# A hybrid decoder step: the input stage in another order, xT stored in parts, the scratch read back in four transfers

## The chip, the core and the metric

The kernel runs on one core of a Trainium2 chip. The metric is the device time of one execution in microseconds (us). Three runs of the kernel before give the time; one further execution was recorded by the hardware profiler, and all rows below come from that one. TensorE multiplies, VectorE (DVE), ScalarE (ACT) and GpSimd (POOL) do the elementwise work, SyncE (SP) issues most transfers; an engine works through its instructions in the order in which they were written. PSUM is the memory that TensorE writes.

## What is computed

One layer of a decoder for 256 prompt rows and 8 sample rows that share all weights, in float32:

```python
h = rmsnorm(x, norm_mix)
proj = h @ w_in                       # q, k, v, z, pooling input, two gates, decays
pool_out = pool_mixer(proj[...])      # trailing window means, 4 groups
qkv = silu(short_conv(proj[...]))     # causal depthwise conv, 4 taps
o = gated_delta_chunked(q, k, v, g, beta, state)
merged = gate_pool * (pool_out @ w_pool_up) + gate_gdn * (o_gated @ w_gdn_up)
x = x + merged @ w_o
gu = rmsnorm(x, norm_ffn) @ w_gate_up
x = x + (silu(gu[..., :D_FF]) * gu[..., D_FF:]) @ w_down
x = x + (p_l @ w_ple) * sigmoid(x @ w_ple_gate)
y = rmsnorm(x, norm_final)
```

The model width is 2048, with 16 heads of 128; the outputs are y for both groups and the new pooling, conv and delta-rule states.

## The kernel before

**Layout.** Activations are held transposed: 128 channels on the partitions, 16 such tiles (`KT`), and 264 columns, the 256 prompt rows and the 8 sample rows. Each float32 product is made of three fast ones: both operands are split into a high part (`wh`, `hh`) and a rest (`wl`, `hl`), and high by high, high by rest and rest by high are summed in PSUM.

**Weights.** `stream` lists all weight blocks in order, 512 KB each. `wload` (L431) issues the transfer of the next into one of three `wr` buffers on SP; `wsplit` (L443) has ScalarE copy it to `wh` and VectorE, or GpSimd when the planner finds it free, subtract to `wl`; four buffers of each. `wblock` (L457) hands the next split block to a gemm. `gemm` (L471) runs over blocks, and between its products calls `tick`.

**Order.** All order is written by the program. `Model` (L34) keeps an estimated time for each engine while the instructions are generated, and `tick` (L260) advances other work, in the form of generators, when the estimate says that its data is there: `paced` ones at every tick, `main` one after another, `post` and `lanes` side by side. A generator that yields -1 is resumed when the estimate of its last work is reached, one that yields a tuple at that time. `Model.run` adds 7 us to a large transfer that ScalarE issues (L147).

**Input.** `load_x` (L616) issues x in seven pieces, the sample rows, and the first three weight blocks. `input_norm` (L632) transposes 16 groups of channels (`xt` in PSUM, copied to `xT`), with the squares of each quarter of x on ScalarE and VectorE after the group's second transpose. Then VectorE sums them, GpSimd takes the power (L383), TensorE spreads the factor over the columns (`rb`) and ScalarE copies it to `rx`. `htile` (L670) makes one tile: VectorE multiplies to `xn`, ScalarE copies to `hh`, VectorE subtracts to `hl`; the last one also issues the store of all of `xT` to DRAM (`xd`, read again as the residual much later). One weight block and four tiles are made ahead of the first gemm, the rest inside it.

**First gemm and conv.** `qkv` (L796) with `wide` set makes the keys of the first four heads with four PSUM banks at a time, 8 blocks of 24 products; the next gemm makes the queries. After each the generator steps `a` (ScalarE: last tap, and the rows for the state), `b` (VectorE: the other taps) and `d` (SiLU) read the bank, so it comes free when the taps are done. `conv_state` (L580) prepares the sample rows' conv and at its end copies two rows of the state from DRAM to DRAM.

**Delta rule.** For each of four head groups `gdn_a` (L871) builds triangular matrices and inverts their diagonal blocks on GpSimd. It writes 32x32 blocks to DRAM (`scr`, four transfers of 32 KB on ScalarE's queue), reads them back to `gone` four times over (L970, one transfer of 512 KB), runs 62 steps on GpSimd, and moves the result by way of `scr2` to `Tt`. `gdn_b` follows. `gdn_sample` (L1148) does the sample rows, with `swap` (L1188) storing each state and loading another. `pool_state` (L1329) loads old pooling rows and copies 14 of 15 from DRAM to DRAM, `p_rows` (L1558) loads the rows of p; each transposes at the next resumption. `ffn` (L1521) holds the longest stretch of plain gemms.

Of the kernel before, what the change touches and what calls it, by code (L numbers as in the profile page):

```python
# [14 lines left out]
P = 128  # L15
# [18 lines left out]
class Model:  # L34
# [92 lines left out]
    def run(self, floor=0.0):  # L127
# [5 lines left out]
        for k in range(self.seen, len(lst)):  # L133
            i = lst[k]
            eng = str(i.engine).split(".")[-1]
            if eng not in self.T or type(i).__name__.startswith("Bass"):
                continue
            ins = [b for b in map(self.box, i.ins) if b]
            out = [b for b in map(self.box, i.outs) if b]
            at = max([self.T[eng], floor] + [self.ready(b) for b in ins])  # L140
            if type(i).__name__ == "InstDMACopy":
                self.T[eng] = at + 0.06
                n = max(self.free(b) * (b[2] - b[1]) for b in ins + out) * 4
                end = max(self.ring, at) + n / 320e3
                self.ring = end
                end += 2.3
                if eng == "Activation" and n > 200000:  # L147
                    end += 7.0
                store = out and out[0][5] is None and out[0][0].startswith("out_")
                self.stored = end if store else getattr(self, "stored", 0.0)  # L150
                for b in out:
                    self.wrote(b, end)
                if not store:
                    done = max(done, end)
                continue
            held, more = self.cost(i, ins, out)
            self.T[eng] = at + held
            end = at + held + more
            for b in out:
                self.wrote(b, end)  # L160
            done = max(done, end)
# [4 lines left out]
class Step:  # L166
# [276 lines left out]
    def wsplit(self):  # L443
# [8 lines left out]
        self.sub(lo, raw, hi.bitcast(F32), self.nc.gpsimd if spare else None)  # L452
# [18 lines left out]
    def gemm(self, K, xh, xl, evac, wide=None):  # L471
        M, KS = (2, KB) if wide is None else (4, 2)
        for m0 in range(0, 4, M):
# [7 lines left out]
            for k0 in range(0, K, KS):  # L481
                nk = min(KS, K - k0)
                wh, wl = self.wblock()
                for m in range(M):
                    if wide is not None:
                        if m % 2 == 0 and k0 + 4 + m // 2 < K:
                            self.htile(k0 + 4 + m // 2)
                        elif (m == 1 or k0 > 7) and m % 2 and len(self.pre) < 3:
                            if not self.raws:
                                self.wload()  # L490
                            self.wsplit()
# [88 lines left out]
    def conv_state(self):  # L580
# [32 lines left out]
        self.dma(o["conv_s"][0, :, 0:2, :], i["state_conv"][0, :, 1:3, :])  # L613
# [18 lines left out]
    def input_norm(self, x, xs):  # L632
# [6 lines left out]
        for c in range(4):  # L639
            for k in range(4 * c, 4 * c + 4):  # L640
                t = self.ps("xt")[:, :NT]
                for b in range(2):
                    self.tr(t[:, b * P:(b + 1) * P], x[:, b, k * P:(k + 1) * P])
                cc = (k % 8) * P
                self.tr(t[:, TP:NT], xs[k // 8][:, cc:cc + P])
                if k % 4 == 3:
                    nc.vector.tensor_copy(self.xt[:, k], t)
                else:
                    self.copy(self.xt[:, k], t)
                if k % 4 == 1:  # L650
                    cs = slice(c * 512, c * 512 + 512)
                    xc = (c % 2) * 512
                    self.act(sqj[:, :512], x[:, 0, cs], AF.Square, accum_out=ssq[:, 0, c:c + 1])
                    self.stt_sum(sqj[:, 512:1024], x[:, 1, cs], ssq[:, 1, c:c + 1])
                    self.stt_sum(sqj[:NS, 512:1024], xs[c // 2][:, xc:xc + 512], ssq[:NS, 2, c:c + 1])
# [3 lines left out]
        self.powr(r, r, -0.5)  # L659
        p = self.spread_rows(r)  # L660
        self.rx = self.e1("rx")
        self.copy(self.rx, p)
        self.hh = self.B3("hh", F32R)
        self.hl = self.B3("hl", F32R)

    def stt_sum(self, out, a, acc):
        self.nc.vector.scalar_tensor_tensor(out=out, in0=a, scalar=1.0, in1=a, op0=ALU.mult, op1=ALU.mult,
                                            accum_out=acc)

    def htile(self, k):  # L670
        t = self.e1("xn")
        self.stt(t, self.xt[:, k], self.g_mix(k), self.rx, ALU.mult, ALU.mult)
        self.split(self.hh[:, k], self.hl[:, k], t)
        if k == KT - 1:
            self.dma(self.xd, self.xt)
# [120 lines left out]
    def qkv(self, part, hg, dst, wide=None):  # L796
# [5 lines left out]
        def evac(m, ps):  # L802
# [3 lines left out]
            u = ps  # L806
            tap = lambda r: self.stt(y[:, 3 - r:TP], u[:, 0:TP - 3 + r], w(r), y[:, 3 - r:TP])
# [17 lines left out]
            self.then(a, b, d, bank=True)  # L825
# [45 lines left out]
    def gdn_a(self, hg, q, k):  # L871
# [94 lines left out]
        for d in range(4):  # L966
# [3 lines left out]
        self.fast(at.rearrange("p s c -> p (s c)"),  # L970
                  scr.rearrange("d a s c -> (d a) (s c)").unsqueeze(0).broadcast_to([4, 32, 1024]))
# [176 lines left out]
    def gdn_sample(self, pool):  # L1148
# [39 lines left out]
        def swap(hg, h):  # L1188
            self.dma(o["ssm_s"][0, :, hg * GH + h].rearrange("b d e -> d b e"), S.pop((hg, h)))
# [139 lines left out]
    def pool_state(self):  # L1329
# [3 lines left out]
        self.dma(o["pool_s"][0, :, 0:14, :], i["state_pool"][0, :, 1:15, :])  # L1333
        yield -1
# [185 lines left out]

    def ffn(self):  # L1521
        nc = self.nc
        self.lane(self.rbcast())
        for g0, ng in ((0, 4), (4, 4), (8, 3)):
# [33 lines left out]
    def p_rows(self):  # L1558
# [5 lines left out]
        yield -1  # L1564
# [84 lines left out]
    def run(self):  # L1649
# [6 lines left out]
        self.wsplit()  # L1656
        for k in range(4):
            self.htile(k)
# [89 lines left out]
```

## Time and profile before

| | before |
|---|---|
| median of 3 runs | 1960.99 us (1959.58 to 1961.83) |
| the profiled execution | 1956.55 us |
| its span | 1954.8 us |
| TensorE busy in the span | 1887.4 us (97%), 15700 matmuls |
| VectorE, ScalarE, GpSimd busy | 1121.1, 877.3, 523.8 us |
| moved by DMA | 344.92 MB, mean 176 GB/s |
| mean granted TensorE clock | 0.985 |

The span is the time between the first and the last recorded instruction; the profiled execution's own time is 1.75 us longer, and the median of the runs shown 4.4 us longer still. Matmuls overlap, so a busy TensorE is not one at its best pace: the number of matmuls that a stretch holds says more. Times in rows are us from the span's start, durations of single groups in the group view are ns. What stands in brackets behind a row is the idle time of that engine just before it and what ended it.

### The profile page before, as it was taken

To read this page: it belongs to the slowest core of one execution; us is meant where nothing else is said; L and a number is where in the kernel's file an instruction comes from. 1 tells how busy PE (TensorE), PEld (TensorE's weight loads), DVE (VectorE), ACT (ScalarE), POOL (GpSimd) and SP (SyncE) were. 2 spreads that over 40 slices of the span, in tenths; PEclk is the share of its full clock that TensorE was granted. 3 is DMA by queue.
4 is the path that set the end of the run, shared out by engine and by line. 5 is a ranking of instruction groups with operands and counts; after the bars stand their busy time and mean duration, and the time that the engine had idled before them with its cause. 6 is when DMAs were issued, how large, how long until landed. Compare 5 with 4: busy or idle time off the path is not lost.

```text
span 1954.8 us, 38004 instructions
## 1 busy us (share of the span) xinstructions
PE 1887.4 (97%) x15700; PEld 1856.6 (95%) x15700; DVE 1121.1 (57%) x1592; ACT 877.3 (45%) x1478; POOL 523.8 (27%) x562
## 2 busy tenths in 40 slices
PE   7789999999999899999999999999999999999997
PEld 5788999999999889999999999999999999999997
DVE  5556557565545966556565555544555545557554
ACT  3454455556544343354354344433444333444444
POOL 1244526363602643412132111100111101113111
PEclk9899999999999999999999999999999999999998
DMA  4546646474657668865655655555655555655553
GB/s 142 170 130 155 179 122 175 129 186 114 189 141 220 179 202 266 247 181 173 212 183 173 185 187 183 180 182 176 188 181 180 183 185 174 184 181 178 168 169 123
DMA packets 367568, 344.92 MB, mean 176 GB/s; under 512 B 26034, under 2 KB 362747, under 8 KB 367251
## 3 DMA queue, kind: packets, MB, share of 16 engines
q1 hardware_dynamic: 354003, 338.82, 57.8%
q10 hardware_dynamic: 13392, 3.67, 1.0%
q8 instruction: 123, 2.02, 0.4%
q14 instruction: 50, 0.41, 0.1%
HBM read 327.28 MB, written 16.03 MB: 176 GB/s over the span
## 4 chain that ended last, share of the span: by engine, by line
PE 81%; DVE 6%; DMA 4%; ACT 4%; issue 2%; POOL 2%; ACTq 0%; SPq 0%; POOLq 0%; DVEq 0%
PE acc L370 75%; DVE wl L341 2%; ACT wh L357 2%; DMA wr<-in_w_in_dram 2%; POOL wl L341 1%; DVE db L341 1%; DMA gone<-scr 1%; DMA wr<-in_w_o_dram 1%; PE pp L370 1%; ACT gset L354 0%; PE kqp L1236 0%; POOL rm L344 0%; PE py L370 0%; PE px L370 0%; DVE dpl L351 0%
## 5 line engine op out<-in xcount | busy, mean ns | idle before, releaser
L341 DVE TENSOR_TENSOR wl<-wr,wh 128x1024 fp32r<-128x1024 f32 x488 | 615.8, 1275 | 571.2 <-ACT wh L357 570.4
L357 ACT ACTIVATE wh<-wr 128x1024 fp32r<-128x1024 f32 x594 | 611.5, 1049 | 483.4 <-PE acc L370 171.7
L370 PE MATMUL acc<-hh,wh 128*128 128x264 f32 x1664 | 490.0, 294 | 18.1 <-DVE k L347 9.3
L370 PE MATMUL acc<-hh,wl 128*128 128x264 f32 x1664 | 479.0, 288 | 12.8 <-POOL wl L341 8.3
L370 PE MATMUL acc<-hl,wh 128*128 128x264 f32 x1664 | 478.8, 288 | 0.0
L341 POOL TENSOR_TENSOR wl<-wr,wh 128x1024 fp32r<-128x1024 f32 x106 | 260.7, 2462 | 738.0 <-ACT wh L357 489.3
L370 PE MATMUL acc<-xnh,wh 128*128 128x264 f32 x1408 | 399.9, 284 | 0.0
L370 PE MATMUL acc<-xnh,wl 128*128 128x264 f32 x1408 | 399.1, 283 | 0.0
L370 PE MATMUL acc<-xnl,wh 128*128 128x264 f32 x1408 | 399.1, 283 | 0.0
L370 PEld LDWEIGHTS acc<-hh,wh 128*128 128x128 f32 x1664 | 320.1, 192 | 22.8 <-issue 11.6
L370 PEld LDWEIGHTS acc<-hh,wl 128*128 128x128 f32 x1664 | 318.9, 192 | 15.1 <-POOL wl L341 9.6
L370 PEld LDWEIGHTS acc<-hl,wh 128*128 128x128 f32 x1664 | 320.1, 192 | 1.5 <-DVE hl L341 0.4
L370 PEld LDWEIGHTS acc<-xnl,wh 128*128 128x128 f32 x1408 | 265.1, 188 | 0.0
L370 PEld LDWEIGHTS acc<-xnh,wh 128*128 128x128 f32 x1408 | 264.9, 188 | 0.0
L370 PEld LDWEIGHTS acc<-xnh,wl 128*128 128x128 f32 x1408 | 264.4, 188 | 0.0
L370 PE MATMUL acc<-hidh,wh 128*128 128x264 f32 x704 | 199.9, 284 | 0.0
L370 PE MATMUL acc<-hidl,wh 128*128 128x264 f32 x704 | 199.6, 283 | 0.0
L370 PE MATMUL acc<-hidh,wl 128*128 128x264 f32 x704 | 199.5, 283 | 0.0
L370 PEld LDWEIGHTS acc<-hidl,wh 128*128 128x128 f32 x704 | 132.5, 188 | 0.0
L370 PEld LDWEIGHTS acc<-hidh,wh 128*128 128x128 f32 x704 | 132.4, 188 | 0.0
L370 PEld LDWEIGHTS acc<-hidh,wl 128*128 128x128 f32 x704 | 132.2, 188 | 0.0
L344 POOL TENSOR_TENSOR gs<-gs,rb 128x264 f32<-128x264 f32 x44 | 33.3, 757 | 365.8 <-ACT gs L354 365.7
(362 smaller groups left out, 2727.7 us busy)
## 6 DMA issues: line engine op xcount, KB each, us to landing
wr<-in_w_in_dram SPq DMA_DIRECT2D x208, 512.0 KB
wr<-in_w_gate_up_dram SPq DMA_DIRECT2D x176, 512.0 KB
wr<-in_w_down_dram SPq DMA_DIRECT2D x88, 512.0 KB
wr<-in_w_gdn_up_dram SPq DMA_DIRECT2D x32, 512.0 KB
wr<-in_w_o_dram SPq DMA_DIRECT2D x32, 512.0 KB
wr<-in_w_ple_gate_dram SPq DMA_DIRECT2D x32, 512.0 KB
S<-in_state_ssm_dram SPq DMA_DIRECT2D x16, 512.0 KB
out_dram<-S SPq DMA_DIRECT2D x16, 512.0 KB
```

The lines of the kernel that those rows point to most:

```text
L341: (eng or self.nc.vector).tensor_tensor(out=out, in0=a, in1=b, op=ALU.subtract)
L344: (eng or self.nc.vector).tensor_tensor(out=out, in0=a, in1=b, op=ALU.mult)
L357: self.nc.scalar.activation(out, a, AF.Copy)
L370: self.nc.tensor.matmul(out, lhsT, rhs, start=start, stop=stop)
```

## The change

Six parts. (1) `input_norm` puts the squares of a quarter ahead of its transposes (the last quarter's ahead of transpose 10), transposes 12 groups, then computes the factor with two weight splits and transposes 12 and 13 around it; the first two splits go to GpSimd by name. Four tiles and a third split follow; transposes 14 and 15 go inside the first gemm, which now splits one block ahead per block. (2) `htile` puts the subtract of a tile behind the multiply and copy of the next. (3) The store of `xT` is a lane of eight transfers, one per 10 us of the planner's time. (4) In the wide gemm ScalarE copies each bank to `u` in SBUF, and the conv reads that. (5) The readback of `scr` is four transfers to 32 partitions each, and the planner's 7 us are gone. (6) The two state copies go to a lane in `ffn`; `swap` waits in the planner's time for the state that it stores; `pool_state` and `p_rows` resume 12 us after their loads.

```diff
@@ Model.run
-                if eng == "Activation" and n > 200000:
-                    end += 7.0
@@ wsplit
-    def wsplit(self):
+    def wsplit(self, eng=None):
...
-        self.sub(lo, raw, hi.bitcast(F32), self.nc.gpsimd if spare else None)
+        self.sub(lo, raw, hi.bitcast(F32), self.nc.gpsimd if spare else eng)
@@ gemm
                     if wide is not None:
-                        if m % 2 == 0 and k0 + 4 + m // 2 < K:
+                        if m % 2 == 0 and k0 + 4 + m // 2 <= K:
                             self.htile(k0 + 4 + m // 2)
-                        elif (m == 1 or k0 > 7) and m % 2 and len(self.pre) < 3:
+                        if m == 1 and k0 < 4:
+                            self.turn(14 + k0 // 2)
+                        if m == 1:
                             if not self.raws:
                                 self.wload()
                             self.wsplit()
@@ conv_state
-        self.dma(o["conv_s"][0, :, 0:2, :], i["state_conv"][0, :, 1:3, :])
@@ input_norm
-        for c in range(4):
-            for k in range(4 * c, 4 * c + 4):
...
-                if k % 4 == 1:
...
+        self.turn = turn
+        for k in range(12):
+            if k in (0, 4, 8):
+                squares(k // 4)
+            if k == 10:
+                squares(3)
+            if k == 8:
+                self.wsplit(nc.gpsimd)
+            turn(k)
         r = self.cp.tile([P, 3], F32, name="rin")
         nc.vector.tensor_reduce(r, ssq, axis=AX.X, op=ALU.add)
         self.ts(r, r, 1.0 / D, EPS, ALU.mult, ALU.add)
         self.powr(r, r, -0.5)
+        self.wsplit(nc.gpsimd)
+        turn(12)
         p = self.spread_rows(r)
+        turn(13)
         self.rx = self.e1("rx")
         self.copy(self.rx, p)
...
+        for k in range(2):
+            self.htile(k)
+        self.wsplit()
+        for k in range(2, 4):
+            self.htile(k)
@@ htile
-        t = self.e1("xn")
-        self.stt(t, self.xt[:, k], self.g_mix(k), self.rx, ALU.mult, ALU.mult)
-        self.split(self.hh[:, k], self.hl[:, k], t)
-        if k == KT - 1:
-            self.dma(self.xd, self.xt)
+        last = self.xn
+        if k < KT:
+            t = self.e1("xn")
+            self.stt(t, self.xt[:, k], self.g_mix(k), self.rx, ALU.mult, ALU.mult)
+            self.copy(self.hh[:, k], t)
+            self.xn = k, t
+        if last:
+            self.sub(self.hl[:, last[0]], last[1], self.hh[:, last[0]].bitcast(F32))
+    def stow(self):
+        for a in range(0, KT, 2):
+            yield (self.now + 10.0,)
+            self.dma(self.xd[:, a:a + 2], self.xt[:, a:a + 2])
@@ qkv
             u = ps
+            if wide:
+                u = self.e1("u")
+                self.copy(u, ps)
...
-            self.then(a, b, d, bank=True)
+            self.then(a, b, d, bank=not wide)
@@ gdn_a
-        self.fast(at.rearrange("p s c -> p (s c)"),
-                  scr.rearrange("d a s c -> (d a) (s c)").unsqueeze(0).broadcast_to([4, 32, 1024]))
+        for c in range(4):
+            self.fast(at[32 * c:32 * c + 32].rearrange("p s c -> p (s c)"), scr.rearrange("d a s c -> (d a) (s c)"))
@@ gdn_sample, swap
+            yield self.at(S[hg, h])
@@ pool_state
-        self.dma(o["pool_s"][0, :, 0:14, :], i["state_pool"][0, :, 1:15, :])
-        yield -1
+        yield (self.now + 12.0,)
@@ ffn
+    def states(self):
+        i, o = self.i, self.o
+        yield (self.now + 60.0,)
+        self.dma(o["conv_s"][0, :, 0:2, :], i["state_conv"][0, :, 1:3, :])
+        yield (self.now + 60.0,)
+        self.dma(o["pool_s"][0, :, 0:14, :], i["state_pool"][0, :, 1:15, :])
...
+        self.lane(self.states())
@@ p_rows
-        yield -1
+        yield (self.now + 12.0,)
@@ run
-        self.wsplit()
-        for k in range(4):
-            self.htile(k)
+        self.lane(self.stow())
```

## Rows read from the trace of the kernel before

**Rows 1.** Windows: stretch, length, busy us (instructions) of PE, PEld, DVE, ACT, POOL; clock, DMA share, GB/s.

```profile
25.00:50.00 25.00, 21.47 (x139) 19.78 (x140) 17.78 (x30) 9.97 (x18) 4.85 (x3) 0.93 0.47 129
50.00:75.00 25.00, 13.76 (x100) 13.07 (x100) 17.40 (x27) 10.66 (x20) 7.61 (x4) 0.80 0.65 229
175.00:200.00 25.00, 19.31 (x134) 18.58 (x132) 12.44 (x18) 9.88 (x18) 11.87 (x23) 0.86 0.65 149
1300.00:1325.00 25.00, 25.00 (x209) 25.00 (x208) 11.17 (x12) 9.55 (x9) 0.00 (x0) 1.00 0.57 176
```

**Rows 2.** Waits of TensorE, whole span: who for whom, us in total, times, longest.

```profile
PE acc L370 <- DVE k L347: 9.3, 1, 9.3
PE gc L370 <- DVE dg L347: 5.4, 1, 5.4
...
PE pt L374 <- DMA prompt_p<-in_p_prompt_dram: 2.0, 1, 2.0
...
PE spt L374 <- DMA sprow<-in_state_pool_dram: 1.6, 1, 1.6
```

**Rows 3.** Timeline, 0 to 30 us: start, duration, engine, line, operation, tiles.

```profile
12.04 0.69 DVE L667 SCALAR_TENSOR_TENSOR sqj<-x 128x512 f32<-128x512 f32 x1 [0.50 <-DMA x<-in_x_prompt_dram]
...
16.25 0.69 PE L374 MATMUL xt<-ident,x 128*128 128x128 f32 x2
...
17.07 0.69 PE L374 MATMUL xt<-ident,x 128*128 128x128 f32 x2
...
18.79 0.85 POOL L383 TENSOR_TENSOR rin<-rin,mhalf 128x3 f32<-128x3 f32 x1 [17.41 <-DVE rin L351]
...
19.69 1.75 PE L370 MATMUL rb<-ident,rin 128*128 128x128 f32 x6 [1.74 <-POOL rin L383]
...
24.98 0.59 PE L370 MATMUL acc<-hh,wh 128*128 128x264 f32 x1 [3.54 <-ACT hh L357]
```

**Rows 4.** Timeline of VectorE and GpSimd in the first gemm.

```profile
30.27 0.43 DVE L341 TENSOR_TENSOR hl<-xn,hh 128x264 fp32r<-128x264 f32 x1 [0.49 <-ACT hh L357]
...
31.27 2.35 POOL L341 TENSOR_TENSOR wl<-wr,wh 128x1024 fp32r<-128x1024 f32 x1 [9.56 <-ACT wh L357]
...
31.60 2.31 DVE L341 TENSOR_TENSOR hl<-xn,hh 128x264 fp32r<-128x264 f32 x1 [0.49 <-ACT hh L357]
...
35.75 1.22 DVE L341 TENSOR_TENSOR wl<-wr,wh 128x1024 fp32r<-128x1024 f32 x1 [0.51 <-ACT wh L357]
```

**Rows 5.** Waits of TensorE, 0 to 160 us.

```profile
PE acc L370 <- POOL wl L341: 5.1, 3, 1.9
```

**Rows 6.** Timeline, 52 to 72 us: SP's queue, ScalarE and TensorE.

```profile
52.66 0.50 SPq L363 DMA_DIRECT2D xd<-xT  x1
...
65.23 1.06 ACT L357 ACTIVATE wh<-wr 128x1024 fp32r<-128x1024 f32 x1 [6.37 <-DMA wr<-in_w_in_dram]
66.20 0.46 ACT L360 ACTIVATE k<-acc,cw 128x264 f32<-128x264 f32 x1
...
71.36 0.56 PE L370 MATMUL acc<-hh,wh 128*128 128x264 f32 x1 [9.32 <-DVE k L347]
```

**Rows 7.** Windows, 55 to 60 us, columns as in rows 1.

```profile
55.00:60.00 5.00, 5.00 (x41) 4.88 (x40) 4.02 (x5) 2.81 (x4) 2.41 (x1) 1.00 1.05 428
```

**Rows 8.** Timeline, 172 to 278 us: the scratch's transfers and who waits for them.

```profile
172.10 1.87 ACTq L367 DMA_DIRECT2D scr<-gset  x4
...
175.71 1.36 ACTq L367 DMA_DIRECT2D gone<-scr  x1
...
188.97 0.24 POOL L344 TENSOR_TENSOR gset<-gone 128x31 f32<-128x31 f32 x1 [9.86 <-DMA gone<-scr]
...
189.73 1.06 ACT L357 ACTIVATE wh<-wr 128x1024 fp32r<-128x1024 f32 x1 [9.16 <-DMA wr<-in_w_in_dram]
...
234.92 0.39 ACTq L367 DMA_DIRECT2D scr<-gone  x1
...
277.26 0.55 ACTq L367 DMA_DIRECT2D gone<-scr  x1
```

## What was predicted

> **What bounds the kernel now.** I read the windows of the engines first. In a stretch of the later matrix stages TensorE is busy all 25.00 us and issues 209 instructions, so one matmul of 264 columns takes 25/209 = 0.12 us and nothing but fewer or faster matmuls would help there [rows 1]. The change adds and removes no matmul, so all it can win is time in which TensorE does not run at that pace. The same view shows where that is: the stretch from 25 to 75 us (13.76 of 25.00 busy in its second half, with a mean granted clock of 0.80), and 175 to 200 us (19.31 busy, clock 0.86) [rows 1]; and nothing of the large products runs in the first 24.98 us [rows 3]. Then I read who TensorE waited for. Four rows touch what is edited: 9.3 us in one wait for the conv taps on VectorE (tile k), 5.4 us in one wait for the decay chain (dg), 2.0 us for prompt_p and 1.6 us for the pool state rows [rows 2]. Last come the timelines of the first 72 us and of the readback of the scratch, which say what was late in each place.
>
> **Input stage.** Before, the 16 transpose groups come first (the last begins at 17.07, one every 0.82), the power on GpSimd starts at 18.79 and takes 0.85, the broadcast takes TensorE 1.75 from 19.69, and the first product of the large gemm starts at 24.98 [rows 3]. After, the last squares stand ahead of the transposes 10 and up, and only 12 groups stand ahead of the factor. What then sets the factor is the arrival of x and GpSimd's order. The third quarter of x lets VectorE start its squares at 12.04, at 0.69 each [rows 3], so two pairs of squares end at 12.04 + 4 x 0.73 = 14.9 if the last quarter is there by 13.4, which no row shows; 17.07 - 3 x 0.82 = 14.6, when transpose 13 began unhindered, is its latest, and that gives 16.1. The power, however, is now queued behind a weight split on GpSimd, 2.35 us each [rows 4], that starts after a ScalarE copy of 1.06 [rows 6] behind the squares of quarter three: 12.04 + 0.69 + 1.06 = 13.8, so GpSimd is free at 16.1. The same split holds up VectorE: while GpSimd ran one from 31.27, a VectorE subtract that took 0.43 just before took 2.31 [rows 4]. If the squares are held up in that way the power starts at about 18.5, if not at 16.4. I take 17.8. Behind it stand 0.85 for the power, 1.75 for the broadcast, 0.82 for transpose 13, two ScalarE copies and three small steps of about 0.4 each: 5.1 us, so the first product starts at 22.9 (21.5 to 23.7), **2.1 us** earlier (1.2 to 3.5).
>
> **First gemm.** It runs from 24.98 to 71.36 - 9.32 = 62.04, 37.1 us, for 192 products that need 192 x 0.12 = 23.0. TensorE waits 5.1 us in it, three times, for weight splits on GpSimd [rows 5], because one block only is split ahead; in the window 25 to 50 it issues 139 instructions of a possible 209, 8.4 us lost, 1.75 of them by the clock (0.93 is half speed for 3.5 us) [rows 1]. With three blocks split ahead (8.6 us of products) a split of 2.35 on GpSimd or 1.22 on VectorE no longer ends last, and with the subtract of a tile put behind the next multiply VectorE does not idle for ScalarE. VectorE then carries per block of 24 products (2.9 us) two tiles of two steps, about 0.4 each as in the subtract's 0.43, and one split at 1.22 [rows 4], 2.8 us in all: just under TensorE, so not all the loss goes. I give back 5.0 of 8.4 (0 to 8.4) and charge 2 x 0.82 = 1.6 for transposes 14 and 15, which now lie inside the gemm: **+3.4 us** (-1.6 to 6.8).
>
> **The stall behind it.** xT's store (2.1 MB) is issued at 52.66 with 384 KB of state copy behind it, and the DMA engines run at 428 GB/s with a share of 1.05 from 55 to 60 [rows 6, 7]. The weight block queued behind them lets ScalarE go on only at 65.23 after 6.37 idle, the conv's first step follows at 66.20, and TensorE gets its banks at 71.36 [rows 6]. After, the store is 8 transfers of 264 KB, 10 us apart on the planner's clock, each 264/428 = 0.6 us of the engines beside a weight stream that leaves room; the state copies go to the feed-forward stage, where TensorE is at its 209 and DMA at a share of 0.57 [rows 1]. SP issues each part when xT has long been written, so nothing waits behind it. The banks are released by one copy of 0.46 per bank on ScalarE instead of by the taps on VectorE. What is late next is that copy behind one weight copy: 0.46 + 1.06 = 1.5. So 9.3 - 1.5 = 7.8, and about 1.5 for the products that ran at half clock after the pause (0.80 in the window [rows 1]): **+9.3 us** (7 to 11).
>
> **Scratch readback.** Four 32 KB stores are issued from 172.10 to 173.97, and the readback that waits for them is issued at 175.71, so four small transfers pass within 3.6 us; the readback of 512 KB reaches GpSimd at 188.97, 13.3 us after its issue [rows 8]. In that time a weight block is held up too: ScalarE idles 9.16 us for it until 189.73 [rows 8], and the window loses 5.69 us [rows 1]. After, it is four transfers of 32 rows with a contiguous source. By the small transfers it should land in 4 to 5 us; by the old one in 13. I take the first, as the row nearest in shape. ScalarE pays three more issues of 0.47 (1.87/4 [rows 8]), hidden, since it is idle there. The first readback then gives back 4.0 of 5.69 (0 to 5.7) and the other three, during which TensorE had splits in hand, 1.0 together. **+5.0 us** (0 to 7.5). The Trainium skill, "DMA: Bandwidth & Descriptors", "Rules for kernel authors", bears on this from both sides: a leading broadcast of c copies keeps a DMA on at most c engines, which would make the old readback a matter of 4 engines; and it says of two transfers to partition halves "Don't bother", by which the split alone gives nothing and the time would be that of the second rival below. The 13.3 us agree with the first, and nothing here shows the second.
>
> **Other waits.** The loads of pool state and prompt rows are given 12 us before their transposes: 3.6 us of waits [rows 2], of which **+3.0** (0 to 3.6). The decay chain's 5.4 us depends on which splits GpSimd has at that time, and the planner will choose anew: half, **+2.5** (-3 to 5.4). The state store behind a time (swap), the new argument of the split and the removed penalty in the planner cost no instruction; they only move others: 0 (-3 to 3).
>
> **Sum.** 2.1 + 3.4 + 9.3 + 5.0 + 3.0 + 2.5 = 25.3. The profiled execution took 1956.55 (span 1954.8), the median is 1960.99, so the same sum gives 1931.2 there and **1935.7** at the median.
>
> **Rivals.** (a) GpSimd's splits become the new wait. They hold VectorE as in [rows 4], three more stand in the opening, and the taps now read u from SBUF beside y. Then the power starts at 18.5, the gemm gains nothing net of the transposes, and the gain is 1.2 - 1.6 + 9.3 + 2.5 + 3.0 = 14.4: 1946.6. For it: 2.31 against 0.43. Against: three blocks in hand. The Trainium skill, "SBUF — State Buffer", "SBUF: two separate sides", speaks for it: GpSimd and a VectorE instruction with two SBUF inputs exclude each other for the whole instruction, and squares, taps and multiplies are of that kind. The subtract's row agrees with it. (b) The readback is bound by its bytes or its small rows, not by its form, and still lands after 13 us: 25.3 - 5.0 = 20.3, 1940.7. For it: DMA share 0.65 over that window already [rows 1]. (c) The stall keeps its length: the eight parts and the weight loads collide, or ScalarE's copies stand behind a late weight block. Then 16.0, 1945. Against: 0.6 us each. (d) Slower: the four readbacks run one after another at 13 us each, 52 instead of 13.3. From the issue at 175.71 to the store of the inverse at 234.92 pass 59 us and the next group's readback is issued at 277.26 [rows 8], so 42 us are to spare; from a landing of about 55 us on every group's chain is the bound, and beyond that each of four groups pays the excess. At 65 us it is 4 x 10 = 40 us lost against 20.3 won: 1980. Against: four small stores within 3.6 us.
>
> **How the numbers follow.** Forecast case 0.56 (its own range 1924 to 1945 from the bounds of the terms), (a) 0.20, (b) 0.12, (c) 0.08, (d) 0.04. To leave out no more than 2 in 10 the range runs from 1920 (all terms near their best ends, 41 us) to 1950, past (a), (b) and (c). About 0.2%, 4 us, is what a measurement of this kernel can tell from no change. Slower by that needs (d): 0.04. Within it needs (a) together with (c), 0.03. Faster: 0.93.
>
> **What would show it.** Input stage: first product of tile hh at 21.5 to 23.7. Gemm: no wait for wl over 1 us in it. Stall: no TensorE gap over 2 us between the first and second gemm, and that second gemm running by 56 us, 15 us earlier than 71.36. Readback: GpSimd's wait for it at 5 us or less each, and no ScalarE wait of 9 us for a weight block. Others: the rows for prompt_p and sprow gone. The prediction is wrong if the gaps vanish and new ones of like size stand in the decay or mixer stages, where the planner's order changes though the code does not.

## The result, and the profile of the kernel after

| | before | after |
|---|---|---|
| median of the runs | 1960.28 us (1955.97 to 1961.83, 4 runs) | 1930.81 us (1925.40 to 1932.39, 4 runs) |
| the profiled execution, its span | 1956.55, 1954.8 us | 1929.83, 1928.1 us |
| mean granted TensorE clock | 0.985 | 0.989 |

The ratio is 0.9848, with a 95% interval of 0.9823 to 0.9874: **1.5% faster**, 29.5 us by the medians and 26.7 us by the two profiled executions. The forecast was 25.3 us (1935.7 us).

The windows that stood worst in [rows 1], now of the kernel after (columns as there: busy time and instructions of PE, PEld, DVE, ACT and POOL, granted clock, DMA share, GB/s):

```profile
25.00:50.00 25.00, 24.81 (x193) 23.34 (x193) 21.71 (x37) 10.42 (x18) 9.13 (x24) 1.00 0.62 166
50.00:75.00 25.00, 23.98 (x194) 22.69 (x194) 17.62 (x37) 16.03 (x34) 7.37 (x3) 1.00 0.50 133
175.00:200.00 25.00, 25.00 (x205) 24.74 (x204) 16.23 (x25) 13.74 (x27) 15.50 (x28) 1.00 0.68 194
```

TensorE issues 193, 194 and 205 instructions of a possible 209 in them, and the granted clock in them is 1.00 (2.4 GHz), where it was 0.93, 0.80 and 0.86. The list of TensorE's waits over the whole span, to be held beside [rows 2 and 5]:

```profile
PE kqp L1266 <- DMA S<-in_state_ssm_dram: 11.1, 7, 3.4
PE rb L368 <- POOL rin L381: 2.9, 1, 2.9
PE acc L368 <- DVE q L345: 1.9, 1, 1.9
PE acc L368 <- POOL wl L339: 1.7, 2, 0.9
PE gc L368 <- DVE dg L345: 1.4, 1, 1.4
```

The waits for the taps (k), for prompt_p and for sprow are gone, dg has fallen from 5.4 to 1.4, wl in the first gemm from 5.1 to none. New at the top is kqp, 11.1 us in seven places, in the sample stage; it was 2.0 us in one place before.

**Where the gain arises along the way.** Each trace holds 15700 matmuls. 14130 of them are products of the large gemms (tile acc), and these come in the same order in both kernels. So the start of the n-th product can be compared; the difference is what after is ahead.

| product | place | before, us | after, us | ahead |
|---|---|---|---|---|
| 192 | last of the first gemm | 61.8 | 54.4 | 7.4 |
| 240 | second gemm | 78.5 | 60.2 | 18.3 |
| 912 | before TensorE is held up by the first readback | 183.6 | 162.4 | 21.3 |
| 1056 | after it | 211.2 | 182.3 | 28.9 |
| 3912 | early in the sample stage | 647.5 | 619.5 | 28.0 |
| 4824 | late in it | 793.6 | 772.5 | 21.1 |
| 5952 | before the prompt rows | 934.8 | 912.4 | 22.4 |
| 6432 | behind the prompt rows | 998.2 | 971.7 | 26.5 |
| 10080 | feed-forward | 1442.8 | 1416.3 | 26.5 |

So 7.4 us come from the input stage and the first gemm, 10.9 from the stall, 3.0 on the way from there to the first readback, 7.6 about that readback, 5.6 are lost in the sample stage, and about 4 come back where the prompt rows were waited for.

### The profile page after: what moved, and what is told of

It is laid out like the page before. It is cut to its first block, busy times and chain, and to the rows that moved or that the text cites. A ratio compares the mean times of both kernels' runs of the same rounds, so it can differ in the third digit from the quotient of the medians.

```text
span 1928.1 us, 38025 instructions
## 1 busy us (share of the span) xinstructions
PE 1881.3 (98%) x15700; PEld 1853.6 (96%) x15700; DVE 1128.0 (59%) x1594; ACT 880.9 (46%) x1484; POOL 521.2 (27%) x560
## 4 chain that ended last, share of the span: by engine, by line
PE 85%; DVE 6%; DMA 4%; ACT 2%; issue 2%; POOL 1%; SPq 0%; ACTq 0%; POOLq 0%; DVEq 0%
PE acc L368 79%; DVE wl L339 1%; ACT wh L355 1%; DMA out_dram<-S 1%; DVE sw L336 1%; DMA S<-in_state_ssm_dram 1%; POOL wl L339 1%; DMA wr<-in_w_in_dram 1%; DVE k L345 1%; PE pp L368 0%; PE py L368 0%; PE kv L372 0%; PE px L368 0%; DVE S L345 0%; PE pS L368 0%
## 5 line engine op out<-in xcount | busy, mean ns | idle before, releaser
L339 DVE TENSOR_TENSOR wl<-wr,wh 128x1024 fp32r<-128x1024 f32 (+1 forms) x490 | 620.5, 1279 | 529.8 <-ACT wh L355 528.1
L339 POOL TENSOR_TENSOR wl<-wr,wh 128x1024 fp32r<-128x1024 f32 x104 | 256.6, 2470 | 705.8 <-ACT wh L355 425.0
L342 POOL TENSOR_TENSOR gs<-gs,rb 128x264 f32<-128x264 f32 x44 | 33.3, 757 | 365.8 <-ACT gs L352 365.8
```

The source lines that it names most:

```text
L339: (eng or self.nc.vector).tensor_tensor(out=out, in0=a, in1=b, op=ALU.subtract)
L342: (eng or self.nc.vector).tensor_tensor(out=out, in0=a, in1=b, op=ALU.mult)
```

## The experiments

All are the kernel after with one thing taken back, except where it says otherwise. "Ahead" is read as in the table above. Ratios are to the kernel before; one that lies inside or overlaps 0.9823 to 0.9874 can't be told from the kernel after.

**The store of xT, the taps, and both.**

```diff
@@ run (first and third run)
-        self.lane(self.stow())
@@ htile, behind the last tile (first and third run)
+        if k == KT - 1:
+            self.dma(self.xd, self.xt)
@@ conv (second and third run)
-            if wide:
-                u = self.e1("u")
-                self.copy(u, ps)
-            self.then(a, b, d, bank=not wide)
+            self.then(a, b, d, bank=True)
```

> The changed kernel with xT stored in one transfer of 2.1 MB when the last tile is made, as before; all else as changed. Theory A (the store and the banks stalled TensorE together): a weight block queued behind the store lands about 2.1 MB / 428 GB/s = 5 us late, but three split blocks (8.6 us of products) are in hand and the banks are freed by ScalarE's copies, so 0 to 2 us are lost: 1931 to 1933 us. Theory B (the store alone was the stall): TensorE waits 7 to 9 us again behind the first gemm: 1938 to 1940 us.

> The changed kernel without the copies to u: the taps of the first gemm read the PSUM banks, which come free when VectorE is done; the store stays in parts. Theory A: VectorE needs about 1.9 us per bank and the next gemm opens with two banks, so TensorE waits 3 to 4 us once between the first two gemms: 1934 to 1935 us. Theory B (the store alone was the stall): no wait over 1 us there, 1931 us.

> Both undone: one store of 2.1 MB, and the banks held by the taps. Theory A: the weight block late behind the store holds ScalarE's queue, the taps behind it start late and TensorE waits 7 to 9 us: 1938 to 1940 us, more than the two alone add up to. Theory B: as with the store alone. If instead the three blocks in hand had removed the stall by themselves: 1931 to 1933 us.

Measured: 1934.98 us with the whole store (0.9867, 0.9841 to 0.9893), 1932.89 with the taps from the bank (0.9858, 0.9831 to 0.9885), 1935.78 with both (0.9873, 0.9851 to 0.9895). Both together cost 5.0 us by the medians, with intervals that still overlap, where the stall was forecast at 9.3. The first and the third time lie between the theories, the second below theory A and above theory B. From the third run's list of TensorE's waits:

```profile
PE gc L368 <- DVE dg L345: 5.6, 1, 5.6
PE acc L368 <- DVE k L345: 2.9, 1, 2.9
```

The wait for the taps is 2.9 us and not the 9.3 of [rows 2], and the third run is 13.3 us ahead at product 240, 5.0 less than after. The whole store alone brings back no pause between the two gemms at all (18.3 us ahead at product 240, as after); what it costs stands behind them, in waits of 2.9 for wabl and 5.4 for dg. So the pause of 9.3 us had two parts: a late weight block ahead of ScalarE's step, and the bank tied to the taps, 2 to 3 us of waiting (2.2 in the second run, 2.9 in the third). With the new input stage the first part is gone whichever way xT is stored. Three things that differ there were not separated: more blocks are in hand, the store is issued at 41.46 and not at 52.66, and the state copies no longer stand behind it.

**The old input stage in the new kernel.** Input order, tiles and the schedule of splits in the first gemm as before; the rest new.

In words, for the code is that of the kernel before: 16 groups and then the factor, one block split, no subtract put off.

> The changed kernel with the input stage of before: 16 transposes with the squares among them, one block split and four tiles made ahead, a tile's subtract right behind its copy, splits in the first gemm as before; store in parts, copies to u and all else as changed. Theory A (terms one and two of the prediction): 2.1 + 3.4 = 5.5 us lost, 1936 us, with the first product at 25.0 us and waits for GpSimd's splits in the first gemm. Theory B (GpSimd's two early splits hold VectorE and eat the gain of the new order): 1930 to 1932 us.

Measured: 1945.71 us (0.9925, 0.9902 to 0.9948), 14.9 us more than after and 10 more than either theory. The first product starts at 24.97, the first gemm ends 1.4 us behind the kernel before, and these waits are back:

```profile
PE acc L368 <- POOL wl L339: 7.3, 5, 1.9
PE gc L368 <- DVE dg L345: 5.5, 1, 5.5
PE ab L368 <- DVE wabl L339: 2.9, 1, 2.9
```

At product 240 it is 9.1 us ahead, so the new store and taps, with the copies moved, do bring the forecast 9 us when the old stage stands before them (10.5 from the end of the first gemm). The input stage is worth 8.8 us up to the end of the first gemm (7.4 ahead against 1.4 behind) and 14.9 in all: the waits for wabl (2.9) and dg (5.5 against 1.4) stand in its wake. The decay chain is on time only in the kernels that have the input stage, the store and the taps all new; why was not tried by itself.

**One readback, and two.** The source of all four forms has the same 32 rows of 4 KB, and 512 KB are written.

```diff
-        for c in range(4):
-            self.fast(at[32 * c:32 * c + 32].rearrange("p s c -> p (s c)"), scr.rearrange("d a s c -> (d a) (s c)"))
@@ one
+        self.fast(at.rearrange("p s c -> p (s c)"),
+                  scr.rearrange("d a s c -> (d a) (s c)").unsqueeze(0).broadcast_to([4, 32, 1024]))
@@ two
+        for c in range(2):
+            self.fast(at[64 * c:64 * c + 64].rearrange("p s c -> p (s c)"),
+                      scr.rearrange("d a s c -> (d a) (s c)").unsqueeze(0).broadcast_to([2, 32, 1024]))
```

> As the kernel after, but each readback of the scratch is again one transfer of 512 KB with the broadcast in front (the planner's 7 us stay out). Theory: the form of the transfer set its landing. Then it lands 12 to 14 us after its issue in all four head groups (6.4 to 6.9 after, 13.3 before), GpSimd's waits for it go from 2.4 to 4.4 back to 9 to 12 us, a weight block behind it is late again in the first group, and the kernel takes 1935 to 1939 us, 4 to 8 more than after. Rival, the form matters to the landing but not to the time, because TensorE now has splits in hand when the first readback comes: 12 to 14 us of landing, and 1929 to 1933. Rival, what else is in flight set the landing: 6 to 8 us in this form too.

> As the kernel after, but each readback is two transfers to 64 partitions, each with its 32 rows of source broadcast twice. The bytes are the same in all forms. If a leading broadcast of c copies keeps a transfer on few DMA engines, each of the two has no more spread than the old one had and they lie beside each other or one behind the other: landing 13 us or more (up to 26). If the size of one transfer sets the landing, it lies between the two: 8 to 11 us. If only the number of transfers beyond one counts: 6 to 7 us. Time of the kernel: 1931 to 1933 for a landing up to 10 us, 1935 to 1940 for 13 us or more.

Measured: 1945.84 us with one (0.9933, 0.9913 to 0.9952) and 1956.34 with two (0.9984, 0.9972 to 0.9996), which leaves almost nothing of the whole change. The landings came as expected for a form that keeps a transfer on few engines, the times are 7 and 16 us beyond the longest expected. Issue and landing of the first readback, from the timelines of ScalarE's queue and of GpSimd, in the kernel after:

```profile
148.25 1.75 ACTq L365 DMA_DIRECT2D gone<-scr  x4
155.51 0.24 POOL L342 TENSOR_TENSOR gset<-gone 128x31 f32<-128x31 f32 x1 [4.05 <-DMA gone<-scr]
```

with one transfer:

```profile
149.20 1.10 ACTq L365 DMA_DIRECT2D gone<-scr  x1
162.80 0.24 POOL L342 TENSOR_TENSOR gset<-gone 128x31 f32<-128x31 f32 x1 [10.22 <-DMA gone<-scr]
163.48 1.06 ACT L355 ACTIVATE wh<-wr 128x1024 fp32r<-128x1024 f32 x1 [7.66 <-DMA wr<-in_w_in_dram]
```

and with two:

```profile
148.62 1.61 ACTq L365 DMA_DIRECT2D gone<-scr  x2
166.13 0.24 POOL L342 TENSOR_TENSOR gset<-gone 128x31 f32<-128x31 f32 x1 [14.20 <-DMA gone<-scr]
162.93 1.06 ACT L355 ACTIVATE wh<-wr 128x1024 fp32r<-128x1024 f32 x1 [7.77 <-DMA wr<-in_w_in_dram]
```

From issue to landing: 7.3, 13.6 and 17.5 us. Two transfers are slower than one, so neither the size of a transfer nor their number explains it. What does is seen by queues. ScalarE's queue is q10, and the row gives its packets, MB and share of the 16 DMA engines while the readback ran: with one transfer (151 to 162), with two (151 to 165.6) and in the kernel after (150 to 154.6).

```profile
q10 hardware_dynamic: 131, 0.52, 21.0%
```

```profile
q10 hardware_dynamic: 131, 0.52, 10.3%
```

```profile
q10 hardware_dynamic: 192, 0.52, 43.7%
```

The same 0.52 MB kept 3.4, 1.6 and 7.0 engines busy on the mean. Its 128 packets of 4 KB took 10.7, 14.6 and 4.3 us, and in the trace at most 6, 4 and 17 of them are under way at once. So a readback that copies its source c times, c being 4 and 2, runs on about c engines. The weight block behind it comes late with it (ScalarE idle for 7.66 and 7.77), and after the one transfer has ended, what is left of the weights (q1) runs on 27.1% of 16, 4.3 engines (162.2 to 165):

```profile
q1 hardware_dynamic: 283, 0.26, 27.1%
```

TensorE stands still for it and then runs at half clock, here with one transfer (first two lines) and with two:

```profile
162.00:163.00 1.00, 0.00 (x0) 0.00 (x0) 0.00 (x0) 0.00 (x0) 0.20 (x1) 1.00 0.26 87
166.00:167.00 1.00, 1.00 (x5) 1.00 (x6) 0.96 (x4) 0.36 (x1) 0.81 (x3) 0.50 0.15 33
```

```profile
161.00:162.00 1.00, 0.00 (x0) 0.00 (x0) 0.00 (x0) 0.00 (x0) 0.00 (x0) 1.00 0.13 51
165.00:166.00 1.00, 0.71 (x3) 0.71 (x4) 1.00 (x4) 0.00 (x0) 0.00 (x0) 0.50 0.13 45
```

This agrees with the Trainium skill, "DMA: Bandwidth & Descriptors", "Rules for kernel authors", by which a leading broadcast of c copies keeps a DMA on at most c engines; the same section's "Don't bother" on transfers to partition halves does not hold where the split removes that broadcast (7.3 us against 13.6). In both runs the planner's 7 us stay out, so it places later work as if the readback landed early; how much of the 15.0 and 25.5 us is owed to that was not tried.

**One part alone: four readbacks in the kernel before.** The same edit the other way round, and the 7 us of the planner taken out.

> The kernel before with one part of the change alone: each readback of the scratch as four transfers (and the planner's 7 us for it gone). In the kernel after, giving the old form back cost 15 us, and in the 12 us before the old readback landed the share of the DMA engines fell to 0.27 with 90 GB/s. Theory: the form takes the same time in both kernels, so the part alone brings 10 to 15 us here: 1945 to 1950, with landings of 6 to 8 us in all four groups. Rival, the prediction's sum: the part is worth 5 us in the kernel before, because three of its four readbacks stand where TensorE has blocks in hand, and the 15 us come only with the other parts: 1953 to 1957.

Measured: 1951.20 us (0.9967, 0.9954 to 0.9980), 8.4 less than the 1959.58 of the kernel before beside it: between the two expectations. It lands 5.3 to 6.2 us after the first issue in the four groups, for example in the first (issue and landing):

```profile
L365 ACTq DMA_DIRECT2D gone<-scr x4: 323/444/587, 177.2 to 178.7; - x4
182.92 0.24 POOL L342 TENSOR_TENSOR gset<-gone 128x31 f32<-128x31 f32 x1 [2.21 <-DMA gone<-scr]
```

It is behind by 1.6 us at product 912 and ahead by 4.6 at 1056 and by 7.8 at 1824, so the first readback gives 6.2 and the second some 3; with the later two the lead ends at 7.0. In the kernel after, going back to one transfer costs 8.3 us at product 1056 (20.6 ahead, not 28.9), 1.1 of it from before the readback, and 16.7 by 3912 (11.3, not 28.0), and the waits for weight blocks stand at the first, the third and the fourth readback. In the list of that run (one transfer, rest as after):

```profile
PE acc L368 <- ACT wh L355: 7.6, 3, 3.8
```

The kernel after has no such wait. So the part is worth 8.4 us in the one kernel, where the planner's 7 us went with it, and the old form costs 15.0 in the other, where the planner does not allow for it; 5.0 was too low in both.

**Eight readbacks.** Each of 64 KB to 16 partitions.

```diff
-        for c in range(4):
-            self.fast(at[32 * c:32 * c + 32].rearrange("p s c -> p (s c)"), scr.rearrange("d a s c -> (d a) (s c)"))
+        for c in range(8):
+            self.fast(at[16 * c:16 * c + 16].rearrange("p s c -> p (s c)"),
+                      scr.rearrange("d a s c -> (d a) (s c)")[16 * (c % 2):16 * (c % 2) + 16])
```

> As the kernel after, but each readback is eight transfers of 64 KB to 16 partitions each instead of four of 128 KB. If the landing is still set by how the transfer is cut, it falls from 6.4 to 7 us to 4 to 5, GpSimd's waits of 2.4 to 4.4 us fall by 1 to 2 each, and the time stays within 2 us of the kernel after (1928 to 1932), since TensorE waits for nothing there any more. If bytes and the weight blocks beside it set it, the landing stays at 6 to 7 us, and four more issues of 0.4 us on ScalarE's queue are paid on top: landing 7 to 8.5 us, time 1930 to 1933.

Measured: 1938.09 us (0.9905, 0.9888 to 0.9921), worse than either expectation. ScalarE's timeline in the first group, and the eight issues by themselves (shortest, median and longest in ns):

```profile
147.99 6.72 ACTq L365 DMA_DIRECT2D gone<-scr  x6
154.81 0.42 ACT L352 ACTIVATE v<-v 128x264 f32<-128x264 f32 x1 [6.02 <-DMA wr<-in_w_in_dram]
155.29 1.04 ACT L355 ACTIVATE wh<-wr 128x1024 fp32r<-128x1024 f32 x1
```

```profile
L365 ACTq DMA_DIRECT2D gone<-scr x8: 308/378/444, 146.1 to 154.4; - x8
```

The last six issues hold ScalarE for 6.72 us, where four took 1.75; the weight copy behind them starts at 155.29 instead of 152.97 (after), and the landing comes 8.0 to 11.1 us after the first issue. An issue is no dearer than before, 0.31 to 0.44 us. The rest is two pauses, from 149.4 to 152.25 and from 153.0 to 154.40. In the trace the issue behind each pause waits for a semaphore, the counter that tells of a transfer's landing, which it shares with a weight block that SyncE issued earlier; those blocks land at 152.22 and 154.37, 0.03 us before the issues. So the price of an issue, 0.4 us, did carry to eight. What the expectation left out is that a transfer can have to wait for an unrelated one whose semaphore it is given.

**State copies and loads in their old places.**

```diff
-        self.lane(self.states())
@@ conv_state, pool_state: the two copies back at their old places
@@ pool_state, p_rows
-        yield (self.now + 12.0,)
+        yield -1
```

> As the kernel after, but the two state copies stand where they stood before, and the loads of pool state and prompt rows are followed at once by their transposes, as before. By the prediction's term for these (3.0 us; the waits for prompt_p and sprow were 2.0 and 1.6 us) the kernel takes 1933 to 1935 and the two waits are back in TensorE's list. Rival, the copies moved to the feed-forward stage cost there what they saved here, and the waits come back in smaller size, since other blocks are in hand: 1929 to 1932. Against both: the 384 KB copy beside the parts of the store brings the stall behind the first gemm back, 1936 or more.

Measured: 1938.66 us (0.9902, 0.9881 to 0.9924), 7.9 more than after and above the 1933 to 1935 expected. The two waits are back:

```profile
PE spt L372 <- DMA sprow<-in_state_pool_dram: 3.5, 1, 3.5
PE pt L372 <- DMA prompt_p<-in_p_prompt_dram: 2.4, 1, 2.4
```

That is 5.9 us of the 7.9; in the kernel before they were 3.6 [rows 2]. The other 2.0 are not accounted for. Along the way the run is 0.5 us behind after at product 3456, ahead of the pool rows, and 7.7 at 3648, behind them (21.2 ahead, not 28.9), but only 2.0 at 5952 (20.4, not 22.4), and 6.1 behind the prompt rows. The copy beside the parts of the store brings no stall (17.4 us ahead at product 240 against 18.3 in after, and 0.8 of the difference stands at the first product): moving that one was of no use to the first stage.

**The sample stage: storing each state at once.**

```diff
         def swap(hg, h):
-            yield self.at(S[hg, h])
```

> As the kernel after, but the sample stage stores each state as soon as the generator comes to it, as before, instead of waiting in the planner's time for it. Theory: the sample stage gives back 8 us of the lead because its state loads come too late behind those delayed stores (TensorE waits for S of in_state_ssm 11.1 us in seven places after, 2.0 us in one before). Then these waits fall below 4 us and the kernel takes 1922 to 1927 us. Rival, the 8 us are the limit of the DMA engines, which are full in this stage (share 1.07 and over after), or of SyncE's own waits: the state waits stay within 3 us of 11.1 or turn into waits for weight blocks, and the time is 1929 to 1935.

Measured: 1928.17 us (0.9840, 0.9824 to 0.9855), 2.6 less than after by the medians, too little to tell apart. TensorE's wait for the states in this run (it is 11.1 in after), and SyncE's queue's waits for a state to be ready to store, first of this run and then of after (570 to 800 us):

```profile
PE kqp L1265 <- DMA S<-in_state_ssm_dram: 6.1, 2, 3.5
SPq L361 <- DVE S L345: 33.3, 9, 11.8
```

```profile
SPq L361 <- DVE S L345: 5.5, 5, 2.0
```

The new wait in `swap` does what it is for: without it SyncE stands 33.3 us in front of stores that are not ready, with it 5.5. TensorE's wait for the states falls from 11.1 to 6.1 when it is taken out, but other waits come in their place, for weight blocks (4.3) and for VectorE (1.7), and nothing is won: this run goes from 28.7 us ahead at product 3912 to 22.3 at 5952, after from 28.0 to 22.4. Nor are the loads of the states later in after; the last four are issued at 738.7 to 756.8 there and at 748.3 to 767.2 here. The expectation of 1922 to 1927 fell, and with it the theory that the delayed stores cost the stage its lead; the rival, by which the waits turn into waits for weight blocks, is nearer.

The runs suggest where to look instead. The two that keep the old loads and state copies lose only 0.8 us (the run above with old copies and loads) and 1.6 (the kernel before with four readbacks) between products 3912 and 5952, all others 3.2 to 8.2. So the loss seems to go with the new places of the loads and copies, which had gained more than that just before (7.2 us between products 3456 and 3648). What in the stage takes it is open.

**Who splits the first two weight blocks.**

```diff
@@ wsplit (both runs)
-        self.sub(lo, raw, hi.bitcast(F32), self.nc.gpsimd if spare else eng)
+        self.sub(lo, raw, hi.bitcast(F32), eng if eng is not None else (self.nc.gpsimd if spare else None))
@@ input_norm (both runs)
             if k == 8:
-                self.wsplit(nc.gpsimd)
+                self.wsplit(nc.vector)
@@ behind the power (first run only)
-        self.wsplit(nc.gpsimd)
+        self.wsplit(nc.vector)
@@ gdn_sample, swap (second run only)
-            yield self.at(S[hg, h])
```

> As the kernel after, but the first two weight splits of the opening are made by VectorE (1.22 us each unhindered) and not by GpSimd (2.35). After, VectorE's square of 512 columns took 2.81 us beside GpSimd's first split, and the power on GpSimd came at 17.34. If that lock is what holds up the opening, the power starts by 16.5 and the first product at 21.3 to 22.0, and the kernel is 0.5 to 1.5 us faster than after. Rival, GpSimd's splits cost the opening nothing net, since VectorE pays 2.4 us for the two: first product at 22.5 or up to 2.4 us later, and the time 1930 to 1934.

> As the kernel after, but only the first weight split of the opening is made by VectorE, the second stays on GpSimd behind the power, and the sample stage stores each state at once as before. With both splits on VectorE the power began at 16.48 instead of 17.34, but it then took 1.76 us instead of 0.85, since the second split ran on VectorE beside it, and the first product came at 22.60 as ever. Theory: GpSimd and VectorE held each other up in both orders. Then here the power begins at 16.4 to 16.6 and takes 0.85 again, the first product begins at 21.6 to 21.9, and with the 2 us of the sample stage the kernel takes 1926 to 1929 us. Rival: the first product does not hang on the power (ScalarE's rx, the tiles or a weight copy are later): first product at 22.3 or later, and 1928 to 1931.

Measured: 1929.12 us with both splits on VectorE (0.9851, 0.9827 to 0.9875) and 1928.80 with the first alone and the swap at once (0.9833, 0.9812 to 0.9855); neither can be told from after. The timelines can. The opening in the kernel after:

```profile
13.02 2.35 POOL L339 TENSOR_TENSOR wl<-wr,wh 128x1024 fp32r<-128x1024 f32 x1 [11.64 <-ACT wh L355]
13.10 2.81 DVE L648 SCALAR_TENSOR_TENSOR sqj<-x 128x512 f32<-128x512 f32 x1
17.34 0.85 POOL L381 TENSOR_TENSOR rin<-rin,mhalf 128x3 f32<-128x3 f32 x1 [1.98 <-DVE rin L349]
22.56 0.59 PE L368 MATMUL acc<-hh,wh 128*128 128x264 f32 x1 [1.75 <-ACT hh L355]
```

with both splits on VectorE:

```profile
16.30 1.23 DVE L339 TENSOR_TENSOR wl<-wr,wh 128x1024 fp32r<-128x1024 f32 x1
16.48 1.76 POOL L381 TENSOR_TENSOR rin<-rin,mhalf 128x3 f32<-128x3 f32 x1 [15.10 <-DVE rin L349]
22.60 0.59 PE L368 MATMUL acc<-hh,wh 128*128 128x264 f32 x1 [1.75 <-ACT hh L355]
```

and with the first alone:

```profile
16.89 0.85 POOL L381 TENSOR_TENSOR rin<-rin,mhalf 128x3 f32<-128x3 f32 x1 [15.51 <-DVE rin L349]
22.10 0.59 PE L368 MATMUL acc<-hh,wh 128*128 128x264 f32 x1 [1.75 <-ACT hh L355]
```

The square that takes 0.69 alone [rows 3] takes 2.81 beside GpSimd's split; turn it round, and the power that takes 0.85 alone takes 1.76 beside VectorE's split, so the first product does not move. With one split each, neither is held, and the first product comes 0.46 us sooner, although x came later there (VectorE's square of the third quarter began at 11.93 and not at 11.65). That is between the theory (21.6 to 21.9) and its rival (22.3 or later). So each of the two engines holds the other up, and that is worth half a microsecond here. This last kernel has the lowest median but one; that it beats the kernel after is not shown.

## Why the prediction was right, and where its sum was not

The time was forecast at 1935.7, in a range of 1920 to 1950; 1930.81 came. By its terms:

**Input stage, +2.1.** First product at 22.56 (22.9 forecast, 21.5 to 23.7), 2.4 us sooner. The power began at 17.34 (17.8 forecast, with the square held up by the split): the middle road was the right one. From there to the first product it took 5.2 (5.1 forecast, though the five steps of 0.4 with the three terms before them add up to 5.4).

**First gemm, +3.4.** Measured 7.4 - 2.4, 4.9 before rounding, inside the range. TensorE's only waits there, behind the first product, are for hl, 1.0 us in two places; none is for a split. So the term was right in kind and somewhat under-sized. In its wake the decay chain's wait fell too, so undoing the whole opening costs 14.9.

**The stall, +9.3.** 10.9 along the way, at the upper end of 7 to 11. But it was priced as if it belonged to the store and the taps alone; undoing those costs 5.0, since the new input stage covers most of the stall by itself. The sum stayed near, because each stall was counted once. That the late weight block would go with the input stage, whichever way xT is stored, was not seen.

**Readback, +5.0.** The landing was forecast at 4 to 5 us and took 6.4 to 7.3 from the first issue in the four groups, against 11.9 to 14.0 before. GpSimd's wait for it is 4.1, 4.4 and 2.4 us in the first three groups, below the 5 that were to show it, and 12.1 in the fourth, 5 of it from before the issue. What was mis-sized is the worth: 4.0 at the first and 1.0 for the three others together. It was 7.6 about the first, and undoing the form costs 15.0. That "TensorE had splits in hand" in the later groups was read from the kernel before; in the kernel after, a late readback makes it wait at the third and the fourth too. Rival (b) fell: the bytes are the same at 7.3, 13.6 and 17.5 us.

**Other waits, +3.0.** Both waits are gone; 7.9 by undoing, 5.9 of it in these two waits. **Decay, +2.5.** The wait fell from 5.4 to 1.4, and 3.0 us are won between products 240 and 912. It is back at 5.4 to 5.6 in the four experiments that undo the input stage, the store or the taps, and stays at 1.6 in the two that move the splits; that it was the planner's choice is plausible and not shown.

**What was missing** is a term for the sample stage, where 5.6 us of the lead are lost. The swap, costed at nothing with 3 on either side, is not it: undoing it leaves the lead behind the stage where it was (22.3 against 22.4).

**Luck in the sum.** Along the way the places that were priced brought 2.4, 4.9, 10.9, 7.6 and 3.0 us, and about 4 came at the prompt rows: 33 where 25.3 were forecast. The loss that had no term, and 0.9 between products 1056 and 3912, brought it back to 26.5. So the mechanisms were right, and the nearness of the total is in part two errors of opposite sign.

**Rivals.** (a) In its sum (14.4) the readback's 5.0 was left out, so it stood for 1941.6 rather than 1946.6. GpSimd's splits do hold VectorE. Beside the square there are the taps, which now read two operands from SBUF; from the timelines of VectorE and GpSimd in the kernel after:

```profile
61.57 5.63 DVE L345 SCALAR_TENSOR_TENSOR k<-u,cw,k 128x254 f32<-128x254 f32 x3
67.23 1.40 DVE L345 SCALAR_TENSOR_TENSOR k<-u,cw,k 128x254 f32<-128x254 f32 x3
```

```profile
61.44 2.44 POOL L339 TENSOR_TENSOR wl<-wr,wh 128x1024 fp32r<-128x1024 f32 x1 [7.23 <-ACT wh L355]
64.12 2.40 POOL L339 TENSOR_TENSOR wl<-wr,wh 128x1024 fp32r<-128x1024 f32 x1 [0.24 <-ACT wh L355]
```

Three taps take 5.63 us while two splits run and 1.40 when none does. This agrees with what the Trainium skill, "SBUF — State Buffer", "SBUF: two separate sides", says of VectorE instructions with two SBUF inputs. But the taps hold no bank any more, so nothing waits for them; in the opening the lock costs half a microsecond, and in the first gemm, with three blocks in hand, TensorE waits for no split. (c) did not come: no pause between the gemms. (d) had no ground: no readback took longer than 7.3 us.

The terms undone one by one (14.9, 5.0, 15.0, 7.9; the swap can't be told from nothing) sum to 43, the gain is 29.5. So the parts are not a sum in either direction: two of them cover the same stall (store and taps, and the input stage), and others are worth more with the rest in place (the readback, 15.0 against 8.4).

## What to carry to other kernels

A transfer that repeats its source in the outermost dimension is worth trying as so many plain transfers: look for a queue whose share stays under c/16 while everything waits for it. An edit ahead of a stall can also cover the stall; so price two edits that remove the same pause once, together, and read what covers a stall from the kernel as it will be, not as it is. And judge an edit by the lead behind its stage, not by one wait in it: the wait for the states fell from 11.1 to 6.1 us and nothing was won.

## What the runs showed of the hardware that was not expected

One readback of 512 KB with its source repeated four times kept 3.4 of 16 DMA engines busy on the mean, and in two halves repeated twice 1.6, so that cutting it in two made it slower (17.5 against 13.6 us), while four plain pieces kept 7.0 busy and took 7.3. Of eight small transfers issued in a row none took longer to issue than 0.44 us, but two had to wait until a weight block of another queue had landed, 2.9 and 1.4 us. And the exclusion between GpSimd and VectorE stretched a three-column power on GpSimd from 0.85 to 1.76 us.
